# A decoder layer on one core: output projection and second feed-forward product by one level of Strassen's scheme

## The chip, the cores and the metric
One core of a Trainium2 chip runs the whole program. The metric is the device time of one execution in microseconds (us), the median of several runs. Engines: PE (TensorE, the matrix engine; its weight loads are listed as PEld), DVE (VectorE), ACT (ScalarE), POOL (GpSimd), SP (SyncE, which issues nearly all DMAs here).

## The reference, cut to what matters
One layer (DEPTH = 1) of a decoder with 512 tokens, model width 1024 and feed-forward width 4096, all in float32:
```
h = rms_norm(x, norm1_g)
A, B, C, D = four mixers of h, each of width 512
merged = sum over the four of sigmoid(gate_i(h)) * (mixer_i @ w_branch[i])    # 512 x 1024
x = x + merged @ w_out                                                        # output projection, 1024 x 1024
h2 = rms_norm(x, norm2_g)
x = x + relu(h2 @ w_ff1)**2 @ w_ff2                                           # 1024 x 4096, then 4096 x 1024
```
The change touches the last three lines only.

## The kernel before, in words
**Three matmuls for one.** A float32 operand is split into a rounded part (hi) and a rest (lo): ACT copies it into the rounded type (line 84), DVE subtracts that from the original (line 85; with a factor lines 88 and 89). `mm3` then issues hi*hi, hi*lo and lo*hi, the lines 143 to 145. Every one of these matmuls has 128x128 stationary weights and 512 moving columns.

**Weights.** `plan` lists all weight units in the order of use. A unit is 128x1024 numbers (512 KB). `load_raw` issues its DMA on SP into a ring of three `raw` tiles, `load_w` splits it into rings of three `whi` and three `wlo` tiles, and `wunit` hands the next one to PE, with the split two units and the DMA five units ahead. A unit feeds 24 matmuls.

**Order of the queues.** The program is written for a tile framework. It places each engine's instructions by a plan of its own, in which what was written first goes first unless it is not ready and something later is; waits and buffers are derived from the tiles. So the written order is not exactly the order on an engine's queue: the loads of x for the residual (line 1129), which are written behind the last branch, are issued while that branch runs.

**The stages that the change touches,** in the order of time:
- `branch(3)`: the last of four branches adds to the eight `merged` tiles (128 channels x 512 tokens each). The product is gated on DVE (line 828), and POOL adds it (line 832).
- Output projection: the eight `merged` tiles are halved and split into `mT` (lines 88 and 89). `gemm_a` runs twice, once for each half c of the 1024 output channels: stationary mT, moving w_out, four PSUM banks, one for each 128 tokens t; 2 x 8 x 4 x 3 = 192 matmuls. DVE adds the banks to the residual x2 (line 1138). The sum is transposed on PE (line 175), scaled by norm2_g and split into `xT`; ACT sums its squares (line 1144).
- First product (FF1): 32 units of `gemm_b`, each with 24 matmuls into one bank (128 of 4096 channels x 512 tokens): 768 matmuls. Then relu on ACT (line 1153) and the square on DVE (line 1154) into the tile `y`.
- Second product (FF2): two passes c over all 32 `y`, each with 16 units. Before a unit two `y` are split into `yy`; 2 x 4 x 3 matmuls accumulate in four banks over the whole pass; 768 matmuls in all. At the end of a pass DVE scales by the row's rms factor and adds x2 (line 1174), and SP writes the rows out.

**Memory.** `yy`, `mg` (merged) and `tg` lie in the pool `pg`, which is allocated from the right end of the memory, as are `xp` and `dnp` before it; all else lies in pools on the left.

Of the kernel before, what the change touches and what calls it, by code (L numbers as in the profile page):

```python
# [11 lines left out]
F32 = mybir.dt.float32  # L12
# [9 lines left out]
P = 128  # L22
S = 512
# [15 lines left out]
def trunk(ctx, tc, x, positions, norm1_g, w_in, dn_conv_w, dn_a_log, dn_dt_bias, dn_out_norm_g,  # L39
# [66 lines left out]
    def load_raw(i):  # L106
        while len(raws) <= min(i, len(plan) - 1):
            srcs, n, width = plan[len(raws)]
# [4 lines left out]
            raws.append(raw)  # L113

    def load_w(i):
        while len(wts) <= min(i, len(plan) - 1):
            j = len(wts)
            load_raw(j)
            used = plan[j][1] * plan[j][2]
            hi = wp.tile([P, 1024], F32R, tag="whi", name="whi")  # L120
            lo = wp.tile([P, 1024], F32R, tag="wlo", name="wlo")
            split(hi[:, :used], lo[:, :used], raws[j][:, :used])
            wts.append((hi, lo))
# [18 lines left out]
    def mm3(ps, lh, ll, rh, rl, start, stop):  # L142
        T.matmul(out=ps, lhsT=lh, rhs=rh, start=start, stop=False)  # L143
        T.matmul(out=ps, lhsT=lh, rhs=rl, start=False, stop=False)  # L144
        T.matmul(out=ps, lhsT=ll, rhs=rh, start=False, stop=stop)  # L145

# [34 lines left out]
    def mm4(lhsT, rhs):  # L181
# [163 lines left out]
    plan += plan_branch(3)  # L345
    for c in range(2):
        plan += spec_a(w_out[0], [(c * 512, 512)])
    for m in range(32):
        plan += spec_b(w_ff1[0], m * P)
    for c in range(2):  # L350
        for u in range(16):
            plan += spec_a(w_ff2[0, u * 256:(u + 1) * 256], [(c * 512, 512)], 2)
    load_w(AHEAD - 1)
# [765 lines left out]
    mT = []
    for k in range(KC):  # L1120
        hi, lo = WR("m", ("G", "V", "R", "U")[k // 2])
        split_scaled(hi, lo, merged[k], 0.5)
        mT.append((hi, lo))
    x2 = []
# [7 lines left out]
    ss2 = small([NT, 2], "ss2")  # L1132
    xb = [[up.tile([P, 4, S], F32R, tag="h", name="xT", bufs=4) for _ in range(2)] for _ in range(2)]
    xT = [tuple(xb[k // 4][i][:, k % 4, :] for i in range(2)) for k in range(KC)]
    for c in range(2):
        banks = gemm_a(512, mT)
        for t in range(NT):
            V.tensor_tensor(out=x2[t][c], in0=x2[t][c], in1=banks[t], op=ALU.add)
        for k in range(4):
            pb = tpose([x2[t][c][:, tsl(k)] for t in range(NT)])  # L1140
            split_scaled(*xT[c * 4 + k], pb, par(R_G2 + c * 4 + k))
        for t in range(NT):
            s_ = W("sq")
            A.activation(out=s_, in_=x2[t][c], func=AF.Square, accum_out=ss2[:, t, c:c + 1])
    r2 = small([NT], "rstd2")
    V.tensor_tensor(out=r2, in0=ss2[:, :, 0], in1=ss2[:, :, 1], op=ALU.add)
    V.tensor_scalar(out=r2, in0=r2, scalar1=1.0 / D, scalar2=EPS, op0=ALU.mult, op1=ALU.add)
    V.reciprocal(out=r2, in_=r2)
    ys = []
    for m in range(32):  # L1150
        ps, = gemm_b(xT)
        y = W("y", "AQSSGVRU"[m // 4])
        A.activation(out=y, in_=ps, func=AF.Relu)
        V.scalar_tensor_tensor(out=y, in0=ps, scalar=0.0, in1=y, op0=ALU.max, op1=ALU.mult)  # L1154
        ys.append(y)
    for c in range(2):
        cs_ = slice(c * 512, (c + 1) * 512)
        banks = [gbank() for _ in range(NT)]
        for u in range(16):
            hi, lo = wunit()  # L1160
            yy = []
            for kk in range(2):
                yh, yl = (pg.tile([P, S], F32R, tag="mg", name="yy", bufs=8) for _ in range(2))
                split(yh, yl, ys[u * 2 + kk])
                yy.append((yh, yl))
            order = [(kk, t) for kk in range(2) for t in range(NT)]
            if u == 15:
# [40 lines left out]
```

## Time and profile before
| | us |
|---|---|
| median of 3 runs | 1054.85 |
| lowest and highest run | 1054.62, 1056.58 |
| span of the profiled execution, first to last instruction | 1054.5 |
| PE busy in it | 1031.2 |
| DVE, ACT, POOL busy | 533.2, 401.3, 171.5 |

The profiled execution is known by its span; the median of the runs lies 0.4 us above it. A PE that is busy all the time can still be slowed, since the ends of its matmuls are modelled: what counts is the distance from the start of one matmul to that of the next.

### The profile page before, as it was taken

How to read it: one execution, taken by the hardware profiler on the slowest of the kernel's cores; microseconds unless marked ns; L12 is line 12 of the kernel's file. 1: busy time of each engine (PE TensorE's matmuls, PEld its weight loads, DVE VectorE, ACT ScalarE, POOL GpSimd, SP SyncE). 2: the span in 40 equal slices, each digit the busy share in tenths (PEclk: the TensorE clock that was granted, in tenths of full speed). 3: DMA queues.
4: the chain of work that ended last, by engine and by line, in shares of the span. 5: the costliest groups of instructions: out<-in, count | busy, mean ns of one | idle time of the engine just before them, and what ended most of it. 6: DMA issues, size and time to landing. Idle time of an engine off the chain costs nothing.

```text
span 1054.5 us, 13053 instructions
## 1 busy us (share of the span) xinstructions
PE 1031.2 (98%) x5067; PEld 847.4 (80%) x5067; DVE 533.2 (51%) x894; ACT 401.3 (38%) x700; POOL 171.5 (16%) x206
## 2 busy tenths in 40 slices
PE   7989999999999999999999999999999999999998
PEld 6868777888888767778888888888888888888886
DVE  6884899523645854442556334354333334445443
ACT  6572333332434442443444233343222223434331
POOL 2453234100300610104342212000000000000000
PEclk9999989999999999999999999999999999999999
DMA  6334342222233222222422333323333322324221
GB/s 196 102 100 119 91 94 67 81 60 80 71 85 99 76 80 80 61 79 77 126 61 79 121 91 90 99 82 98 100 100 100 94 90 98 100 87 133 100 80 40
DMA packets 130886, 96.71 MB, mean 92 GB/s; under 512 B 15924, under 2 KB 112256, under 8 KB 130824
## 3 DMA queue, kind: packets, MB, share of 16 engines
q1 hardware_dynamic: 130744, 95.85, 31.4%
q8 instruction: 40, 0.66, 0.2%
q14 instruction: 22, 0.18, 0.1%
q10 hardware_dynamic: 80, 0.03, 0.0%
HBM read 92.96 MB, written 2.90 MB: 91 GB/s over the span
## 4 chain that ended last, share of the span: by engine, by line
PE 86%; DVE 8%; issue 2%; DMA 1%; ACT 1%; POOL 1%; SPq 0%; DVEq 0%; ACTq 0%; POOLq 0%
PE g L143 25%; PE g L145 25%; PE g L144 25%; PE m L879 2%; PE m L175 1%; DVE wlo L85 1%; PE m L184 1%; PE m L1025 1%; DVE cv L516 1%; PE m L869 1%; PE m L1093 1%; PE m L1024 1%; DVE D L626 1%; DVE h L89 1%; DMA x<-in_x_dram 1%
## 5 line engine op out<-in xcount | busy, mean ns | idle before, releaser
L85 DVE TENSOR_TENSOR wlo<-raw,whi 128x1024 fp32r<-128x1024 f32 (+2 forms) x160 | 204.8, 1280 | 305.4 <-ACT whi L84 296.1
L84 ACT ACTIVATE whi<-raw 128x1024 fp32r<-128x1024 f32 (+2 forms) x160 | 167.8, 1048 | 368.6 <-PE g L144 235.1
L143 PE MATMUL g<-h,whi 128*128 128x512 f32 x416 | 168.0, 404 | 0.0
L145 PE MATMUL g<-h,wlo 128*128 128x512 f32 x416 | 164.2, 395 | 0.0
L144 PE MATMUL g<-h,whi 128*128 128x512 f32 x416 | 163.6, 393 | 0.0
L144 PE MATMUL g<-wlo,yy 128*128 128x512 f32 x256 | 101.1, 395 | 0.0
L145 PE MATMUL g<-whi,yy 128*128 128x512 f32 x256 | 101.1, 395 | 0.0
L143 PE MATMUL g<-whi,yy 128*128 128x512 f32 x256 | 101.0, 395 | 0.0
L143 PE MATMUL g<-xT,whi 128*128 128x512 f32 x256 | 99.7, 389 | 0.0
L144 PE MATMUL g<-xT,whi 128*128 128x512 f32 x256 | 99.6, 389 | 0.0
L145 PE MATMUL g<-xT,wlo 128*128 128x512 f32 x256 | 99.6, 389 | 0.0
L145 PEld LDWEIGHTS g<-h,wlo 128*128 128x128 f32 x416 | 79.0, 190 | 16.7
L143 PEld LDWEIGHTS g<-h,whi 128*128 128x128 f32 x416 | 79.1, 190 | 16.2 <-issue 0.5
L144 PEld LDWEIGHTS g<-h,whi 128*128 128x128 f32 x416 | 78.9, 190 | 16.1 <-issue 0.5
L85 DVE TENSOR_TENSOR yy<-y,yy 128x512 fp32r<-128x512 f32 x64 | 44.2, 691 | 82.1 <-ACT yy L84 81.7
L84 ACT ACTIVATE yy<-y 128x512 fp32r<-128x512 f32 x64 | 40.4, 631 | 107.2 <-PE g L144 101.5
L832 POOL TENSOR_TENSOR mg<-mg,tg 128x512 f32<-128x512 f32 x24 | 35.7, 1488 | 194.2 <-DVE tg L828 152.8
L145 PEld LDWEIGHTS g<-whi,yy 128*128 128x128 f32 x256 | 48.0, 187 | 11.8
L143 PEld LDWEIGHTS g<-whi,yy 128*128 128x128 f32 x256 | 48.0, 187 | 11.8 <-DVE y L1154 0.2
L144 PEld LDWEIGHTS g<-wlo,yy 128*128 128x128 f32 x256 | 48.0, 187 | 11.6
L143 PEld LDWEIGHTS g<-xT,whi 128*128 128x128 f32 x256 | 48.1, 188 | 10.0
L145 PEld LDWEIGHTS g<-xT,wlo 128*128 128x128 f32 x256 | 48.1, 188 | 10.0
(361 smaller groups left out, 1668.3 us busy)
## 6 DMA issues: line engine op xcount, KB each, us to landing
raw<-in_w_in_dram SPq DMA_DIRECT2D x68, 512.0 KB
raw<-in_w_ff_dram SPq DMA_DIRECT2D x64, 512.0 KB
raw<-in_w_branch_dram SPq DMA_DIRECT2D x16, 512.0 KB
raw<-in_w_out_dram SPq DMA_DIRECT2D x8, 512.0 KB
x<-in_x_dram SPq DMA_DIRECT2D x4, 512.0 KB
x<-in_x_dram SPq DMA_DIRECT2D x8, 256.0 KB
out_dram<-x SPq DMA_DIRECT2D x8, 256.0 KB
raw<-in_w_in_dram SPq DMA_DIRECT2D x4, 456.0 KB
```

The costliest lines, as they stand in the source:

```text
L84: A.activation(out=hi, in_=src, func=AF.Copy)
L85: V.tensor_tensor(out=lo, in0=src, in1=hi.bitcast(F32), op=ALU.subtract)
L89: V.scalar_tensor_tensor(out=lo, in0=src, scalar=sc, in1=hi.bitcast(F32), op0=ALU.mult, op1=ALU.subtract)
L143: T.matmul(out=ps, lhsT=lh, rhs=rh, start=start, stop=False)
L144: T.matmul(out=ps, lhsT=lh, rhs=rl, start=False, stop=False)
L145: T.matmul(out=ps, lhsT=ll, rhs=rh, start=False, stop=stop)
L175: T.transpose(out=pb[:, tsl(t)], in_=srcs[t], identity=ident)
L184: T.matmul(out=pb[:, tsl(t)], lhsT=lhsT[:, tsl(t)], rhs=rhs[:, tsl(t)], start=True, stop=True)
L516: V.scalar_tensor_tensor(out=y[:, 3 - k:], in0=ps[:, :n], scalar=par(R_CONV + 12 * k + blkno), in1=y[:, 3 - k:], op0=ALU.mult, op1=ALU.add)
L626: V.tensor_reduce(out=XB[:, r, m0:], in_=xr.rearrange("p c m -> p m c"), axis=AX.X, op=ALU.add, negate=True)
L832: G.tensor_tensor(out=merged[m], in0=merged[m], in1=tgs[b], op=ALU.add)
L879: T.matmul(out=pv[:, tsl(m)], lhsT=vblk(h, j), rhs=pts[n][:, o_ + j * P:o_ + (j + 1) * P], start=(j == 0), stop=(j == i))
```

## The change
**Strassen's scheme (Winograd's form).** The left matrix is cut into 2 x 2 (tokens 0 to 255 and 256 to 511; even and odd blocks of 128 channels), the right one too (even and odd blocks of 128 rows; column halves of 512). Seven products of the parts, and of sums of the parts, take the place of eight. This is done for the output projection (one group `gO`) and for FF2 cut into four blocks of 1024 rows (groups `gF[0]` to `gF[3]`). Each product p runs in two halves f of its 512 rows: a group has 14 units, and a unit has 2 x 2 x 3 = 12 matmuls (24 before).

**Sums.** All sums of parts run on POOL in float32, before the splits: `w_src` forms four sums of weights for each f (128 x 1024 numbers each), `a_sums` three sums of the left matrix and `a_split` a fourth (128 x 512 each). ACT and DVE split the weights of each unit as before (128 x 1024) and, new, the left part for each unit (128 x 512). After product 6 DVE forms u2 and u3 from PSUM, and POOL adds them into six tiles of x2 (128 x 512). The products 2, 5, 4 and 3 are added from PSUM by DVE, two tiles each.

**Order.** The plan of units alternates: the first eight FF1 units, then for each block three units of the block and one of FF1, four times, then the block's last two units and four of FF1. The fourth block's 14 units stand alone at the end. The 14 units of the projection stand alone too. The weights of a group come as four DMAs of 1 MB into tiles of a new pool `fp`, which takes the place of the pool `up` after the last branch; there is nothing of the projection's sums and splits ahead of the last branch's instructions in the text (`fence`).

**Other parts.** x2 is multiplied by the mean square on POOL (eight tiles) while FF1 runs and by its reciprocal on ACT at the end, so that blocks can add to it at any time. The split left parts lie in `fp`, on the left. The right pools get a pad of 32 bytes each, after which their tiles start at multiples of 64 bytes.

```diff
     def load_w(i):
-        while len(wts) <= min(i, len(plan) - 1):
+        while len(wts) <= min([i, len(plan) - 1] + fence):
             j = len(wts)
             load_raw(j)
+            load_t(j)
...
+            if srcs_w[j] is not None:
+                split(hi.rearrange("p (q c) -> p q c", c=512), lo.rearrange("p (q c) -> p q c", c=512), srcs_w[j])
+                wts.append((hi, lo) + a_split(*plan[j]))
+                continue
...
         load_w(i + AHEAD)
+        load_t(i + AHEAD + 1)
         load_raw(i + AHEAD + AHEAD_RAW)
...
+    PRODS = (1, 7, 6, 2, 5, 4, 3)
+    UNITS = [(1, 0), (7, 0), (1, 1), (7, 1)] + [(p, f) for p in PRODS[2:] for f in range(2)]
...
+    def wload(g, e):
+        for f in range(2):
+            t = fps[0].tile([P, 2, 1024], F32, tag="r" + "eo"[e], name="r" + "eo"[e], bufs=2)
+            SY.dma_start(out=t, in_=g["w"][f * 512:(f + 1) * 512].rearrange("(q e p) c -> e p q c", e=2, p=P)[e])
+            g["eo"[e]].append(t)
+
+    def w_src(g, p, f):
+        e, o = g["e"][f], g["o"][f]
+        b11, b12, b21, b22 = e[:, :, 0:512], e[:, :, 512:1024], o[:, :, 0:512], o[:, :, 512:1024]
+        if p == 7:
+            g["T3"][f] = fps[0].tile([P, 2, 512], F32, tag="T3", name="T3", bufs=2)
+            G.tensor_tensor(out=g["T3"][f], in0=b22, in1=b12, op=ALU.subtract)
+            return g["T3"][f]
+        if p == 6:
...
+            G.tensor_tensor(out=g["T2"][f], in0=g["T3"][f], in1=b11, op=ALU.add)
+            return g["T2"][f]
+        if p == 5:
+            G.tensor_tensor(out=b12, in0=b12, in1=b11, op=ALU.subtract)
+            return b12
+        if p == 4:
+            G.tensor_tensor(out=g["T2"][f], in0=b21, in1=g["T2"][f], op=ALU.subtract)
+            return g["T2"][f]
+        return {1: b11, 2: b21, 3: b22}[p]
+
+    def a_sums(g, f):
...
+        G.tensor_tensor(out=s1, in0=a21, in1=a22, op=ALU.add)
+        G.tensor_tensor(out=a21, in0=a11, in1=a21, op=ALU.subtract)
+        G.tensor_tensor(out=s2, in0=s1, in1=a11, op=ALU.subtract)
...
+    def a_split(g, p, f):
+        y = g["y"][f]
+        if p == 3:
+            G.tensor_tensor(out=g["S2"][f], in0=y[:, :, 1, 0:256], in1=g["S2"][f], op=ALU.subtract)
...
+        ah, al = (fps[0].tile([P, 2, 256], F32R, tag="a" + n, name="a" + n, bufs=4) for n in "hl")
...
+    def wunit_mm(g, p, f, dst, last=None):
+        hi, lo, ah, al = wunit()
...
+        for q in range(2):
+            for t in range(2):
+                mm3(X[t], ah[:, q, tsl(t)], al[:, q, tsl(t)], hi[:, q * 512:(q + 1) * 512],
+                    lo[:, q * 512:(q + 1) * 512], not more and f + q == 0, f + q == 2, more)
...
+            for t in range(2):
+                V.tensor_tensor(out=u[2][t], in0=u[2][t], in1=X[t], op=ALU.add)
+                V.tensor_tensor(out=u[3][t], in0=u[2][t], in1=g["X"][3][t], op=ALU.add)
+            for t in range(2):
+                for d, v in ((dst(2 + t, 1), u[3][t]), (dst(2 + t, 0), u[2][t]), (dst(t, 1), u[2][t])):
+                    G.tensor_tensor(out=d, in0=d, in1=v, op=ALU.add)
...
+    pad(xp, "padx")
...
+    seq = [m for m in range(8)]
+    for i in range(4):
+        us = list(UNITS)
+        for m in range(4 * (i < 3)):
+            seq += [(i,) + us.pop(0) for _ in range(3)] + [8 * i + 8 + m]
+        seq += [(i,) + v for v in us] + [8 * i + 12 + m for m in range(4 * (i < 3))]
...
+    up.release()
+    fps.append(ctx.enter_context(tc.tile_pool(name="fp", bufs=1, reuse_waits="tile")))
+    for e in range(2):
+        wload(gO, e)
...
+    gO["y"] = mgs
+    for f in range(2):
+        a_sums(gO, f)
+    fence.clear()
+    load_w(pos[0] + AHEAD - 1)
+    for p, f in UNITS:
+        wunit_mm(gO, p, f, lambda t, c: x2[t][c])
+        if (p, f) == (3, 0):
+            x2t(0)
...
+            G.tensor_scalar(out=x2[t][c], in0=x2[t][c], scalar1=ms2[:, t:t + 1], scalar2=None, op0=ALU.mult)
...
+    def finish(t, c, ps):
+        A.activation(out=x2[t][c], in_=x2[t][c], func=AF.Copy, scale=r2[:, t:t + 1])
+        V.scalar_tensor_tensor(out=x2[t][c], in0=ps, scalar=r2[:, t:t + 1], in1=x2[t][c], op0=ALU.mult, op1=ALU.add)
+        SY.dma_start(out=out[0, tsl(t), c * 512:(c + 1) * 512], in_=x2[t][c])
...
+            if i < 3 and f == 1 and p in (5, 3):
+                wload(gF[i + 1], int(p == 3))
```

## Rows read from the trace of the kernel before

**Rows 1.** The page: busy times, the granted clock and the DMA rate in 40 slices
```profile
PE 1031.2 (98%) x5067; PEld 847.4 (80%) x5067; DVE 533.2 (51%) x894; ACT 401.3 (38%) x700; POOL 171.5 (16%) x206
...
PEclk9999989999999999999999999999999999999999
...
GB/s 196 102 100 119 91 94 67 81 60 80 71 85 99 76 80 80 61 79 77 126 61 79 121 91 90 99 82 98 100 100 100 94 90 98 100 87 133 100 80 40
```
**Rows 2.** Busy times by stage: projection, FF1, FF2 (stretch, its length, then the engines)
```profile
core 0: us, PE busy (x) PEld busy (x) DVE busy (x) ACT busy (x) POOL busy (x), PEclk, DMA share, GB/s
649.70:695.20 45.50, 45.50 (x210) 37.73 (x209) 18.83 (x22) 16.07 (x27) 2.14 (x1) 1.00 0.32 91
696.90:870.90 174.00, 174.00 (x770) 144.09 (x769) 63.40 (x74) 53.16 (x72) 0.00 (x0) 1.00 0.33 97
870.90:1050.40 179.50, 179.50 (x770) 143.88 (x769) 83.60 (x98) 67.06 (x91) 0.00 (x0) 1.00 0.27 89
```
**Rows 3.** Matmuls by tile (ns min/median/max, first and last start): FF1's, FF2's, projection's
```profile
L143 PE MATMUL g<-xT,whi x256: 389/389/486, 696.9 to 870.5; 128*128 128x512 f32 x128
...
L143 PE MATMUL g<-whi,yy x256: 393/395/407, 871.2 to 1049.7; 128*128 128x512 f32 x128
...
L143 PE MATMUL g<-whi,mh x64: 389/389/477, 649.7 to 694.5; 128*128 128x512 f32 x64
```
**Rows 4.** The chain that ended last, between the projection and FF1
```profile
671.64 1.87 PE m L175 x16
...
695.31 1.88 PE m L175 x16
```
**Rows 5.** Groups by line and shape, 580 us to the end (busy us, mean ns)
```profile
L85 DVE TENSOR_TENSOR wlo<-raw,whi 128x1024 fp32r<-128x1024 f32 x82 | 101.4, 1237 | 165.4 <-ACT whi L84 165.4
...
L84 ACT ACTIVATE whi<-raw 128x1024 fp32r<-128x1024 f32 x82 | 86.5, 1055 | 164.3 <-PE g L144 124.0 <-issue 21.5 <-PE g L145 18.6
...
L85 DVE TENSOR_TENSOR yy<-y,yy 128x512 fp32r<-128x512 f32 x64 | 44.2, 691 | 82.1 <-ACT yy L84 81.7 <-PE g L144 0.4
L84 ACT ACTIVATE yy<-y 128x512 fp32r<-128x512 f32 x64 | 40.4, 631 | 107.2 <-PE g L144 101.5 <-DVE y L1154 5.6
...
L1138 DVE TENSOR_TENSOR x<-x,g 128x512 f32<-128x512 f32 x8 | 5.3, 683 | 2.5 <-PE g L145 2.5
```
**Rows 6.** POOL's largest groups by shape, whole span
```profile
L832 POOL TENSOR_TENSOR mg<-mg,tg 128x512 f32<-128x512 f32 x24 | 35.7, 1488 | 194.2 <-DVE tg L828 152.8 <-issue 41.0 <-DVE rqm L993 0.4
...
L1099 POOL TENSOR_SCALAR E<-Fb,gcc 128x512 f32<-128x512 f32 x4 | 7.2, 1806 | 0.0
```
**Rows 7.** POOL in order of time around 600 us (start, length)
```profile
599.01 1.29 POOL L832 TENSOR_TENSOR mg<-mg,tg 128x512 f32<-128x512 f32 x1 [14.61 <-DVE tg L828]
602.36 2.20 POOL L832 TENSOR_TENSOR mg<-mg,tg 128x512 f32<-128x512 f32 x1 [2.07 <-DVE tg L828]
```
**Rows 8.** DVE in order of time in the same stretch
```profile
601.60 0.68 DVE L828 SCALAR_TENSOR_TENSOR tg<-tg,g 128x512 f32<-128x512 f32 x1
602.20 1.22 DVE L85 TENSOR_TENSOR wlo<-raw,whi 128x1024 fp32r<-128x1024 f32 x1
```
**Rows 9.** POOL, then DVE, around 324 us
```profile
324.39 1.29 POOL L832 TENSOR_TENSOR mg<-mg,tg 128x512 f32<-128x512 f32 x1 [1.38 <-DVE tg L828]
...
324.50 2.26 DVE L85 TENSOR_TENSOR wlo<-raw,whi 128x1024 fp32r<-128x1024 f32 x1 [0.19 <-ACT whi L84]
```
**Rows 10.** POOL, then DVE, around 59 us (line 516 reads one operand from PSUM)
```profile
59.05 1.36 POOL L569 TENSOR_TENSOR UA<-UA,br 128x512 f32<-128x512 f32 x1 [3.90 <-ACT UA L568]
...
59.43 0.74 DVE L516 SCALAR_TENSOR_TENSOR cv<-g,prm,cv 128x511 f32<-128x511 f32 x1
```
**Rows 11.** SP's queue in order of time, 586 to 628 us
```profile
589.39 1.29 SPq L1129 DMA_DIRECT2D x<-in_x_dram  x3
...
619.76 0.37 SPq L112 DMA_DIRECT2D raw<-in_w_branch_dram  x1
624.84 0.37 SPq L112 DMA_DIRECT2D raw<-in_w_out_dram  x1
```
**Rows 12.** The end: the last matmul and the last work of DVE
```profile
1050.15 0.39 PE L145 MATMUL g<-whi,yy 128*128 128x512 f32 x1
...
1050.58 0.75 DVE L1174 SCALAR_TENSOR_TENSOR x<-g,rstd,x 128x512 f32<-128x512 f32 x1 [0.65 <-PE g L145]
```

More of the change, by code (lines that the diff above doesn't have):

```diff
@@ L138, in wunit, with mm3 @@
         load_w(i + AHEAD)
+        load_t(i + AHEAD + 1)
         load_raw(i + AHEAD + AHEAD_RAW)
         return wts[i]
[L142 to L145, printed above, removed]
+    def mm3(ps, lh, ll, rh, rl, start, stop, more=False):
+        T.matmul(out=ps, lhsT=lh, rhs=rh, start=start, stop=False, skip_group_check=more)
+        T.matmul(out=ps, lhsT=lh, rhs=rl, start=False, stop=False, skip_group_check=more)
+        T.matmul(out=ps, lhsT=ll, rhs=rh, start=False, stop=stop, skip_group_check=more)
     def gemm_b(xs, nb=1):
@@ new lines, in wunit_mm @@
+    def wunit_mm(g, p, f, dst, last=None):
+        hi, lo, ah, al = wunit()
+        x = XOF[p]
+        more = p in (2, 4, 3)
+        if not more and f == 0:
+            g["X"][x] = [gbank() if x in (2, 4) else mbank() for _ in range(2)]
+        X = g["X"][x]
+        for q in range(2):
+            for t in range(2):
+                mm3(X[t], ah[:, q, tsl(t)], al[:, q, tsl(t)], hi[:, q * 512:(q + 1) * 512],
+                    lo[:, q * 512:(q + 1) * 512], not more and f + q == 0, f + q == 2, more)
+        if f == 0:
+            return
+        u = g["u"]
+        if p == 1:
+            u[2] = [fps[0].tile([P, 512], F32, tag="u", name="u", bufs=4) for _ in range(2)]
+            for t in range(2):
+                A.activation(out=u[2][t], in_=X[t], func=AF.Copy)
+        elif p == 6:
+            u[3] = [fps[0].tile([P, 512], F32, tag="u", name="u", bufs=4) for _ in range(2)]
+            for t in range(2):
+                V.tensor_tensor(out=u[2][t], in0=u[2][t], in1=X[t], op=ALU.add)
+                V.tensor_tensor(out=u[3][t], in0=u[2][t], in1=g["X"][3][t], op=ALU.add)
+            for t in range(2):
+                for d, v in ((dst(2 + t, 1), u[3][t]), (dst(2 + t, 0), u[2][t]), (dst(t, 1), u[2][t])):
+                    G.tensor_tensor(out=d, in0=d, in1=v, op=ALU.add)
+        elif p != 7:
+            r, c = {2: (0, 0), 5: (2, 1), 4: (2, 0), 3: (0, 1)}[p]
+            for t in range(2):
+                d = dst(r + t, c)
+                if last is None:
+                    V.tensor_tensor(out=d, in0=d, in1=X[t], op=ALU.add)
+                else:
+                    last(r + t, c, X[t])
@@ L187, in trunk, with pad @@
+    def pad(pool, name):
+        G.memset(pool.tile([P, 8], F32, name=name, bufs=1), 0.0)
     W0 = w_in[0]
@@ L345, in trunk @@
     plan += plan_branch(3)
[L346 to L352, printed above, removed]
+    gO = wgroup(w_out[0], 0.5)
+    gF = [wgroup(w_ff2[0, i * 1024:(i + 1) * 1024]) for i in range(4)]
+    fence.append(len(plan) - 1)
+    plan += [(gO, p, f) for p, f in UNITS]
+    seq = [m for m in range(8)]
[4 more added lines that the diff above has]
+        seq += [(i,) + v for v in us] + [8 * i + 12 + m for m in range(4 * (i < 3))]
+    for e in seq:
+        plan += spec_b(w_ff1[0], e * P) if isinstance(e, int) else [(gF[e[0]], e[1], e[2])]
     load_w(AHEAD - 1)
@@ L744, in trunk @@
     pg = tc.alloc_tile_pool(name="pg", bufs=4, side="right")
+    mgs = [pg.tile([P, 2, 2, S], F32, tag="mg", name="mg", bufs=2) for _ in range(2)]
     OB = [W("ob", "U") for _ in range(H)]
@@ L1117, in trunk @@
     branch(3, oD, drain=True)
[L1119 to L1123, printed above, removed]
+    pad(pg, "padg")
+    up.release()
+    fps.append(ctx.enter_context(tc.tile_pool(name="fp", bufs=1, reuse_waits="tile")))
+    for e in range(2):
+        wload(gO, e)
     x2 = []
@@ L1142, in trunk @@
         for t in range(NT):
-            s_ = W("sq")
+            s_ = fps[0].tile([P, S], F32, tag="u", name="sq", bufs=4)
             A.activation(out=s_, in_=x2[t][c], func=AF.Square, accum_out=ss2[:, t, c:c + 1])
[L1145 to L1155, printed above, removed]
@@ L1177, in trunk @@
-    pg.release()
+    gO["y"] = mgs
[7 more added lines that the diff above has]
+            x2t(0)
+    for e in range(2):
+        wload(gF[0], e)
+    x2t(1)
+    pg.release()
+    py = tc.alloc_tile_pool(name="py", bufs=3, side="right", reuse_waits="tile")
+    mr = small([2, NT], "rstd2")
+    ms2, r2 = mr[:, 0, :], mr[:, 1, :]
+    V.tensor_tensor(out=ms2, in0=ss2[:, :, 0], in1=ss2[:, :, 1], op=ALU.add)
@@ new lines, in trunk @@
+    for e in seq:
+        if isinstance(e, int):
+            g, f, q = gF[e // 8], e // 4 % 2, e % 4
+            if q == 0:
+                g["y"].append(py.tile([P, 2, 2, S], F32, tag="y", name="y", bufs=3))
+                if e == 0:
+                    pad(py, "pady")
+            ps, = gemm_b(xT)
+            y = g["y"][f][:, q // 2, q % 2, :]
+            A.activation(out=y, in_=ps, func=AF.Relu)
+            V.scalar_tensor_tensor(out=y, in0=ps, scalar=0.0, in1=y, op0=ALU.max, op1=ALU.mult)
+            if q == 3:
+                a_sums(g, f)
+        else:
+            i, p, f = e
+            wunit_mm(gF[i], p, f, lambda t, c: x2[t][c], finish if i == 3 else None)
+            if i < 3 and f == 1 and p in (5, 3):
+                wload(gF[i + 1], int(p == 3))
```

66 lines of the change are left out of this document (37 added, 29 removed).

## The prediction

> **What bounds the kernel now.** I read the page first: PE is busy for 98% of the span at the full granted clock, DVE for half of it, POOL for 16% [rows 1]. Then the table by stage: the projection takes 45.5 us, FF1 174.0 and FF2 179.5, with PE busy throughout and DVE at 41%, 36% and 47% [rows 2]. So all three stages are as long as their matmuls. For the price of one I took starts, not lengths: FF1's 256 matmuls of one line start from 696.9 to 870.5 us, 765 matmuls further on, which makes 0.2269 us each. FF2's start from 871.2 to 1049.7, which makes 0.2333 [rows 3]. The two differ in the operand held in PE: `yy` in the right pool. The projection, whose `mh` lies on the left, runs at FF1's pace: 192 x 0.2269 = 43.6, and 1.87 for 16 transposes amid it [rows 4] make its 45.5 us. Last I read what the added work will meet: POOL and DVE side by side [rows 7 to 10].
>
> **PE: what is removed.** The projection goes from 192 to 168 matmuls, FF2 from 768 to 4 x 168 = 672. The held operand of both now lies on the left, so I price all at 0.2269. A group of 14 units is 38.1 us. Projection with its transposes: 40.0 (-5.5). FF2: 152.5 (-27.0). If the pace of 0.2333 stayed, FF2 would be 4.3 us longer. By PE alone the change is worth 32.5 us.
>
> **DVE and ACT: what is added.** A unit now has half the matmuls, 2.72 us, and the same weight split. DVE takes 1.24 for the weights and 0.69 for the left part, ACT 1.06 and 0.63 [rows 5]: 1.93 and 1.69 in 2.72 us. Alone, both keep up. The 12 additions from PSUM of a group take 0.68 each [rows 5], 8.2 us.
>
> **POOL: what is added.** A group has 8 sums of 128x1024 and 14 of 128x512 (8 of the left matrix, 6 into x2). One of 128x512 with two inputs takes 1.29 us undisturbed [rows 7]. None of 128x1024 was run: at most twice that, 2.58, and at least twice the 1.15 that remains below when start-up is hidden, 2.30. The Trainium skill (GPSIMD Engine Reference, section 3.1) gives 2.6 cycles an element, by which I estimate 2.2 us; the sums of a group would be under 1 us shorter by it.
>
> **DVE and POOL together.** This is where the sum is decided. POOL's addition took 1.29 us at 599.01 and 2.20 at 602.36 [rows 7], when DVE's split had begun 0.16 us earlier and ended at 603.42 [rows 8]: POOL ran 1.14 us after that end. The other way round, DVE's split began at 324.50 in POOL's addition (324.39 to 325.68) and took 2.26 us, to 326.76 [rows 9]: 1.08 after POOL's end. So these two kinds of instruction, both with two inputs from SBUF, take turns. A DVE instruction with one input from PSUM is not held: 0.74 us within POOL's 1.36 [rows 10]. The Trainium skill (SBUF, section "Who interferes with whom") says the same: DVE with at most one SBUF input does not contend. The trace agrees, so the additions from PSUM are left out below; if they took turns too, a group would be 8.2 us longer.
>
> The price of a turn, net of start-up: 1.08 for a weight split, 0.56 for a left part (0.69 less the same 0.14), 1.15 and 2.30 for POOL's sums. A group: DVE 14 x 1.64 = 23.0, POOL 8 x 2.30 + 14 x 1.15 = 34.5, together 57.5 us of a path that is used by one at a time, against 38.1 on PE. Whether that shows depends on what else PE has.
>
> *Projection.* PE has nothing else: FF1 needs x2. Before the last branch ends little can be done: the left sums of f=0 and the split of the first unit; the other tiles of `fp` lie on the last branch's operands. After it POOL holds 14 sums whose inputs are there (the last merge, 3 left sums, 8 of weights, 2 for product 3): 8 x 2.30 + 6 x 1.15 = 25.3. If each takes turns with one DVE split, only 7 units (11.5) are split after 36.8 us. Then the six additions into x2 (6.9) alternate with three more units (4.9): 48.6. Four units remain for DVE alone (4 x 1.93 = 7.7) with about six additions from PSUM between (4): 60.3. The last unit's matmuls: 63.0 us, that is +17.5 on 45.5. Bounds: turns packed without loss, (34.5 + 1.15 - 3.45) + (23.0 - 1.64) + 2.7 = 56.3 (+10.8); turns that cost nothing, 40.0 and 3 for the start (-2.5); full lengths one after another, 36.1 + 25.1 + 8.2 + 2.7 = 72.1 (+26.6). I take 63: POOL is always ready early, and nothing makes it wait for DVE.
>
> *To FF1.* PE's 16 transposes and FF1's start remain; the last bank must first be added on DVE, which I put at +1 (0 to 3). The mean-square products on POOL (8 x 1.81 [rows 6] = 14.5 us) run in FF1's first eight units (43.6 us), where POOL has little else; uncovered they would cost their length.
>
> *Blocks 0 to 2.* Each has 8 FF1 units beside it: PE 38.1 + 43.6 = 81.7, shared path 57.5 + 8 x 1.08 = 66.1, 81% full. A split may start only when its buffer, three units back, is free, so some come late; I take 1.5 us a block, 4.5 in all. Bounds: 0, and two units a block that wait for one long sum, 2 x 2.3 x 3 = 14.
>
> *Block 3.* No FF1 beside it. Ahead of it are its six left sums (6.9), two weight sums (4.6) and three units (4.9): 57.5 - 16.4 = 41.1 remain, with the last matmuls and a late split some 45 us against 38.1: +6.9. Bounds: 0, and nothing ahead, 60.2 (+22.1).
>
> *DMA and tail.* The bytes are the same; loads come as 1 MB. SP's last load before w_out is issued at 619.76, and it issued loads that are written later already at 589 [rows 11], so 4 MB for the projection, at the 196 GB/s that the first slice shows [rows 1] 21 us, land before 649. Later groups have at least four FF1 units (21.8 us) for their last 2 MB. Uncovered, 1 MB costs 5.3. From the last matmul to the end it was 4.4 us [rows 12]; two tiles instead of one are left then, and ACT's product is done before: 0.
>
> **The sum,** on the span of 1054.5: +17.5 + 1 + 4.5 - 27.0 + 6.9 = +2.9, 1057.4; the median lay 0.4 above the span, so **1058**. The sign hangs on one number: the projection must end within 45.5 + 14.6 = 60.1 us for a gain.
>
> **Rivals.**
> - *Packed turns* (the other side). POOL and DVE still take turns, but no turn falls where PE waits for more than the sum: projection 56.3, blocks 0 to 2 unhindered, block 3 at 41.1. +10.8 + 1 - 27.0 + 3.0 = -12.2, 1043. It decides once the projection is under 60.1. For it: POOL is idle for 84% of the span, and the queues are ordered by readiness [rows 1, 11]. Against it: in the projection all sums are ready at once.
> - *No collision.* The sums find gaps, PE alone decides: -2.5 + 1 - 27.0 = -28.5, 1026. Against it stand both pairs above [rows 7 to 9].
> - *FF1 used up as filler.* PE takes FF1 units ahead whenever a split is late, and block 3 is left with the whole shared path: 52 instead of 45, and 3 us of stall in each earlier block more: +2.9 + 7 + 9, about 1074.
> - *Clock.* Gaps in the projection, where PE works 40 of 63 us, lower the granted clock, which fell only in the first slices [rows 1]. A unit at 1.2 GHz would take 5.4 instead of 2.7 us; with half the units so and half of that behind waits, +9: 1067.
>
> **How the numbers follow.** The forecast (1050 to 1066, its own range) 0.38, packed turns 0.27, no collision 0.12, FF1 as filler 0.13, clock 0.10. No change I can tell is within 0.2% (2.1 us, about what a measurement of this kernel can tell). Slower: 0.23 of the forecast's share and the last two rivals, 0.46; the same: 0.08; faster: 0.07 of the forecast and the first two rivals, 0.46. The 8-in-10 range leaves out most of "no collision" and the far end of "filler": 1034 to 1075.
>
> **What the profile of the changed kernel would show.** Right: 168 matmuls and over 60 us from the last branch to the transposes of c=1; DVE's splits there at 2 to 3.5 us each, ended by POOL's sums; POOL's 128x1024 sums at 2.3 us alone and over 3 in company; FF2's matmuls 0.227 us apart; block 3 some 45 us. Wrong if DVE's splits keep their 1.24 us while POOL works, if the projection is under 56 us, or if PE runs FF1 matmuls amid a block's units so that block 3 is far over 45.

## The result, and the profile after

The changed kernel takes 1086.18 us (median of 4 runs, 1084.36 to 1092.46), the kernel before 1055.45 in the same comparison: ratio 1.0305, 95% interval 1.0286 to 1.0325. Forecast were 1058 and a range up to 1075. The profiled execution has a span of 1082.6 us, 28.1 more than before.

The page of the changed kernel, to be read against [rows 1]:
```profile
PE 1017.7 (94%) x4947; PEld 830.7 (77%) x4947; DVE 672.3 (62%) x966; ACT 437.5 (40%) x746; POOL 410.4 (38%) x328
...
PEclk9999999999999999999999996899999999999899
...
GB/s 195 96 96 127 97 98 60 78 59 78 78 88 97 78 59 78 59 98 117 78 59 117 97 214 0 35 180 94 24 117 136 59 76 177 39 40 195 19 1 78
```
PE did get less to do (120 matmuls fewer in the records), yet the span grew: 65 us without a busy PE where there were 23. The granted clock falls in the slices of the projection, and the DMA rate goes from 214 just before it through 0 and 35 to 180 GB/s.

The same by stage: the projection (from the last branch's end to FF1's first matmul), the first eight FF1 units, block 0 with four FF1 units between its units, the four FF1 units behind its end, the same two rows of block 1, the four FF1 units behind block 2, and block 3:
```profile
core 0: us, PE busy (x) PEld busy (x) DVE busy (x) ACT busy (x) POOL busy (x), PEclk, DMA share, GB/s
648.25:720.30 72.05, 49.03 (x185) 36.24 (x185) 55.78 (x45) 29.16 (x43) 48.63 (x25) 0.83 0.17 60
720.30:765.75 45.45, 45.45 (x210) 37.60 (x208) 26.44 (x29) 18.58 (x30) 32.65 (x17) 1.00 0.33 95
765.75:825.90 60.15, 60.09 (x265) 49.40 (x264) 49.46 (x45) 28.76 (x37) 30.65 (x15) 1.00 0.33 107
825.90:854.20 28.30, 24.12 (x98) 19.16 (x98) 12.98 (x12) 6.74 (x10) 14.87 (x8) 0.94 0.25 72
854.20:914.30 60.10, 60.09 (x266) 49.27 (x265) 49.45 (x45) 28.64 (x37) 30.81 (x15) 1.00 0.33 107
914.30:942.50 28.20, 24.12 (x98) 19.15 (x97) 12.82 (x12) 6.75 (x10) 14.71 (x8) 0.94 0.25 71
...
1002.50:1031.70 29.20, 24.40 (x98) 19.39 (x98) 13.62 (x12) 6.70 (x10) 15.49 (x8) 0.88 0.06 17
1031.70:1078.90 47.20, 41.60 (x169) 32.01 (x167) 38.41 (x35) 23.49 (x32) 24.14 (x13) 0.96 0.09 34
```
The surprise is where PE waits. Amid the interleaved blocks it never does: 264 matmuls in 60.1 us. It waits where four FF1 units stand in a row, plain work that the scheme does not touch: 28.3, 28.2 and 29.2 us for 96 matmuls that take 21.8 at FF1's pace. Against the prediction:

| us | predicted | measured | off by |
|---|---|---|---|
| projection and transposes, to FF1 (47.2 before) | +18.5 | 72.05 + 1.9 - 47.2 - 1.45 = +25.3 | 6.8 |
| PE work of FF2 | -27.0 | -26.75 | 0.2 |
| blocks 0 to 2 | +4.5 | 0.5 amid the units; 6.5 + 6.4 + 7.4 in the four FF1 units: +20.8 | 16.3 |
| block 3 | +6.9 | 47.2 - 38.1 = +9.1 | 2.2 |
| tail | 0 | 3.7 - 4.0 = -0.3 | -0.3 |
| sum | +2.9 | +28.1 | 25.2 |

(1.9 are the transposes of c=1, which now run behind FF1's first matmuls; 1.45 is how much earlier the last branch ends in this execution. The 26.75 are reckoned: FF1 and FF2 took 353.5 us [rows 2], and 1440 matmuls at FF1's pace take 326.75; what the blocks took beyond that stands in their rows.)

The prices of single instructions came out as forecast. DVE's and POOL's groups by shape, 580 us to the end, against [rows 5, 6]:
```profile
L86 DVE TENSOR_TENSOR wlo<-raw,whi 128x1024 fp32r<-128x1024 f32 x42 | 84.0, 2006 | 47.0 <-ACT whi L85 46.6
...
L86 DVE TENSOR_TENSOR al<-y,ah 128x512 fp32r<-128x512 f32 x32 | 34.3, 1071 | 45.4 <-ACT ah L85 45.4
...
L291 DVE TENSOR_TENSOR x<-x,m 128x512 f32<-128x512 f32 x16 | 10.2, 677 | 0.0
```
```profile
L230 POOL TENSOR_TENSOR re<-re 128x1024 f32<-128x1024 f32 x10 | 32.1, 3215 | 0.0
...
L223 POOL TENSOR_TENSOR T<-ro,re 128x1024 f32<-128x1024 f32 x10 | 24.3, 2434 | 71.7 <-DMA ro<-in_w_ff_dram 71.7
...
L249 POOL TENSOR_TENSOR S<-y,S 128x512 f32<-128x512 f32 x8 | 15.6, 1976 | 4.9 <-DVE al L86 4.9
```
DVE's split of 128x1024 takes 2.01 us on average for the 42 units from `raw` and 1.78 over all 112, where it took 1.24; the addition from PSUM keeps its 0.68. POOL's large sum takes 2.4 us undisturbed, within the bounds of 2.30 to 2.58. By the 2.6 cycles an element of the Trainium skill (GPSIMD Engine Reference, section 3.1) I had estimated 2.2 us; the trace is about a tenth above it. But the row of line 223 has another number: POOL sat idle for 71.7 us ahead of four such sums, waiting for a load of `ro`.

One of the four waits, in the order of time of POOL, of SP's queue and DVE, of ACT, and of PE:
```profile
820.48 2.40 POOL L223 TENSOR_TENSOR T<-ro,re 128x1024 f32<-128x1024 f32 x1 [19.84 <-DMA ro<-in_w_ff_dram]
...
829.53 2.40 POOL L223 TENSOR_TENSOR T<-ro,re 128x1024 f32<-128x1024 f32 x1
831.88 1.29 POOL L241 TENSOR_TENSOR S<-y 128x512 f32<-128x512 f32 x1
...
835.48 1.29 POOL L242 TENSOR_TENSOR y<-y 128x512 f32<-128x512 f32 x1
```
```profile
815.23 2.85 SPq L215 DMA_DIRECT2D ro<-in_w_ff_dram  x2
```
```profile
813.93 1.23 DVE L86 TENSOR_TENSOR wlo<-ro,whi 128x1024 fp32r<-128x1024 f32 x1 [0.26 <-ACT whi L85]
...
823.89 0.68 DVE L1301 SCALAR_TENSOR_TENSOR y<-g,y 128x512 f32<-128x512 f32 x1
```
```profile
823.43 1.06 ACT L85 ACTIVATE whi<-raw 128x1024 fp32r<-128x1024 f32 x1 [1.40 <-PE g L162]
836.80 0.63 ACT L85 ACTIVATE ah<-y 128x512 fp32r<-128x512 f32 x1 [12.31 <-POOL y L242]
837.34 1.99 ACT L85 ACTIVATE whi<-raw 128x1024 fp32r<-128x1024 f32 x2
```
```profile
838.43 0.50 PE L160 MATMUL g<-xT,whi 128*128 128x512 f32 x1 [1.44 <-ACT whi L85]
...
841.91 0.50 PE L162 MATMUL g<-xT,wlo 128*128 128x512 f32 x1 [2.74 <-DVE wlo L86]
...
843.04 0.63 PE L162 MATMUL g<-xT,wlo 128*128 128x512 f32 x1
843.47 0.63 PE L160 MATMUL g<-xT,whi 128*128 128x512 f32 x1
```
Read it from below. PE waits for the weights of an FF1 unit. Their split (837.34) starts 13.9 us after the weight split before it (4.2 us in run 5 below); it stands on ACT's queue behind the split of a left part for the next block, which waits 12.31 us for POOL's sum a21 (835.48). That sum's `y` was ready at 824.6, but stands on POOL's queue behind five weight sums of the next block, whose first waits for a 1 MB load; and that load was issued at 815.23 only, when DVE had read block 0's rows out of the first of the two `ro` buffers (813.93). PE needs none of this before block 1, 18 us later. The order is the framework's plan, not the text's: there the left sums come first.

The waits are not the whole price. Behind the second one PE's matmuls start 0.43 us apart (843.04, 843.47) in place of 0.227; the granted clock from 842.5 to 845.5 us is 0.50, which is 1.2 GHz. So of the 20.3 us that the three rows of four FF1 units lose, 13.1 are waits and about 7 the pace behind them.

In the projection PE first waits 10.1 us, from 648.4 to 658.5, with a similar order on ACT and, behind it, on POOL:
```profile
658.46 1.22 PE L160 MATMUL m<-whi,ah 128*128 128x512 f32 x2 [10.08 <-ACT whi L85]
```
```profile
656.83 0.63 ACT L89 ACTIVATE ah<-mg 128x512 fp32r<-128x512 f32 x1 [4.75 <-POOL mg L242]
657.36 1.04 ACT L85 ACTIVATE whi<-re 128x1024 fp32r<-128x1024 f32 x1
```
```profile
657.98 2.80 POOL L223 TENSOR_TENSOR T<-ro,re 128x1024 f32<-128x1024 f32 x1
667.04 1.29 POOL L249 TENSOR_TENSOR S<-mg,S 128x512 f32<-128x512 f32 x1 [6.27 <-DVE al L90]
668.27 3.36 POOL L227 TENSOR_TENSOR T<-T,re 128x1024 f32<-128x1024 f32 x1
```
The first unit's weights (657.36) are split behind four left parts. POOL is later idle for 6.27 us ahead of a sum that only the last product needs, with the sums for the next products behind it.

So there were two theories. **A**: DVE and POOL take turns, and the sum of their work is the path; it was only longer than I made it. **B**: nothing is short of time, but in-order queues hold instructions that wait ahead of others that could run.

### The profile page after: what moved, and what is told of

It reads as the page before. It is cut to its first block, busy times and chain, and to the rows that moved or that the text cites. A ratio compares the mean times of both kernels' runs of the same rounds, so it can differ in the third digit from the quotient of the medians.

```text
span 1082.6 us, 13015 instructions
## 1 busy us (share of the span) xinstructions
PE 1017.7 (94%) x4947; PEld 830.7 (77%) x4947; DVE 672.3 (62%) x966; ACT 437.5 (40%) x746; POOL 410.4 (38%) x328
## 4 chain that ended last, share of the span: by engine, by line
PE 64%; DVE 15%; POOL 8%; issue 7%; DMA 3%; ACT 2%; SPq 0%; POOLq 0%; DVEq 0%; ACTq 0%
PE g L162 16%; PE g L160 16%; PE g L161 16%; DVE wlo L86 6%; POOL T L223 2%; PE m L998 2%; PE m L161 2%; PE m L160 1%; PE m L162 1%; PE m L192 1%; POOL T L227 1%; POOL re L230 1%; PE m L201 1%; DVE al L86 1%; PE m L1144 1%
## 5 line engine op out<-in xcount | busy, mean ns | idle before, releaser
L86 DVE TENSOR_TENSOR wlo<-raw,whi 128x1024 fp32r<-128x1024 f32 (+1 forms) x120 | 187.5, 1565 | 185.0 <-ACT whi L85 175.2
L85 ACT ACTIVATE whi<-raw 128x1024 fp32r<-128x1024 f32 (+1 forms) x120 | 125.2, 1046 | 275.5 <-PE g L161 160.8
L160 PE MATMUL m<-whi,ah 128*128 128x512 f32 x160 | 64.6, 407 | 14.8 <-ACT whi L85 14.8
L161 PE MATMUL m<-wlo,ah 128*128 128x512 f32 x160 | 65.3, 408 | 6.7 <-DVE wlo L86 6.7
L86 DVE TENSOR_TENSOR wlo<-T,whi 128x1024 fp32r<-128x1024 f32 x30 | 48.7, 1625 | 30.4 <-ACT whi L85 30.2
L162 PE MATMUL m<-whi,al 128*128 128x512 f32 x160 | 64.1, 401 | 0.0
L86 DVE TENSOR_TENSOR al<-y,ah 128x512 fp32r<-128x512 f32 x32 | 34.3, 1071 | 45.4 <-ACT ah L85 45.4
L160 PEld LDWEIGHTS g<-xT,whi 128*128 128x128 f32 x256 | 49.2, 192 | 16.1 <-ACT whi L85 6.1
L285 POOL TENSOR_TENSOR x<-x,u 128x512 f32<-128x512 f32 x30 | 51.7, 1761 | 17.5 <-DVE u L281 17.5
L161 PEld LDWEIGHTS g<-xT,whi 128*128 128x128 f32 x256 | 49.3, 193 | 10.6 <-DVE xT L90 0.2
L161 PE MATMUL g<-wlo,ah 128*128 128x512 f32 x120 | 48.2, 402 | 7.1 <-DVE wlo L86 7.1
```

Of the source, the lines that this page charges most:

```text
L85: A.activation(out=hi, in_=src, func=AF.Copy)
L86: V.tensor_tensor(out=lo, in0=src, in1=hi.bitcast(F32), op=ALU.subtract)
L160: T.matmul(out=ps, lhsT=lh, rhs=rh, start=start, stop=False, skip_group_check=more)
L161: T.matmul(out=ps, lhsT=lh, rhs=rl, start=False, stop=False, skip_group_check=more)
L162: T.matmul(out=ps, lhsT=ll, rhs=rh, start=False, stop=stop, skip_group_check=more)
L285: G.tensor_tensor(out=d, in0=d, in1=v, op=ALU.add)
```

## The experiments

There are fourteen more kernels; each ratio is to the kernel before, timed alongside. "Stage" is the projection from the last branch's end to FF1's first matmul, 47.2 us before and 72.1 in the changed kernel; "stretch" the four FF1 units in a row.

**1. No sums.** `w_src` and `a_split` hand out raw parts in place of sums.
```diff
-            G.tensor_tensor(out=g["T3"][f], in0=b22, in1=b12, op=ALU.subtract)
-            return g["T3"][f]
+            return b12
...
```


> The changed kernel without its 64 sums on POOL: products and their splits take the raw parts in place of the sums (the output is not the reference's); order, units, loads, pads, the adds to x2 and everything on PE stay. If the loss comes from the sums alone (their time on POOL, DVE's turns with them, and what waits behind them), PE meets no more than a few us of new idle time: 32.5 us of matmuls gone from 1054.85 and some 3 to 8 us of waits at the stage borders, 1025 to 1031. Rival: the alternation of FF1 and block units, the 1 MB loads or the units of 12 matmuls cost by themselves; then it stays above 1050.

1034.99 us (0.9797, interval 0.9778 to 0.9816), 4 us above the forecast; stage 48.7, stretches without a stall. The sums (they are 80, not the 64 of the text above), with all that they make wait, cost some 50 us. Of the 32.5 us of matmuls 21.3 are gained; the other 11 go to what stayed (units, loads, alternation, the adds to x2), and this run does not part them.

**2. Left sums on DVE.**
```diff
-        G.tensor_tensor(out=s1, in0=a21, in1=a22, op=ALU.add)
+        V.tensor_tensor(out=s1, in0=a21, in1=a22, op=ALU.add)
...
```


> The 40 sums of the left parts (128x512) run on DVE in place of POOL; the same arithmetic. Theory A (DVE and POOL share their turns, and the sum of their work is what PE waits for): the work only changes place, within 4 us of the changed kernel's 1086, since a sum costs DVE at least half of what POOL took. Theory B (an instruction that waits at the head of an in-order queue: the left sums stand on POOL behind weight sums that wait for a load, and ACT's splits of FF1's weights stand behind the split of the left part): the three stretches of four FF1 units fall from 28.2 us to 22 to 23.5 and the time to 1066 to 1074; the start of the projection gains at most 3.

1081.31 (1.0240, 1.0225 to 1.0255): outside both ranges and nearer to A's, against the reading above. The trace says why it tells little: DVE's own plan put these sums behind a split of late FF1 weights, into the burst of POOL's weight sums, where each took 2.2 to 2.9 us and the splits of FF1's weights stood behind them. The stretch kept 27.8 us.

**3. Order pinned as written.** Every weight sum (POOL) and left split (ACT, DVE; all in the form with a factor, 1.0 in the second product) passes through
```diff
+    def KP(g, ins):
+        if True:
+            tc.keep_in_program_order(ins)
...
```


> Nothing but the order of three queues changes: every weight sum on POOL, and every split of a left part on ACT and DVE, is pinned behind what is written before it. Theory A (turns): the same work in another order, 1080 to 1090. Theory B (heads of queues): the left sums no longer stand behind a weight sum that waits for its load, nor the weight splits behind left parts that are not ready: the stretches of four FF1 units fall to 22 to 24 us (-13 to -18), PE's idle time at the start of the projection from 10.3 us to 3 to 6; in all 1058 to 1070. What speaks against a full gain: weight sums issued only three units ahead may come late in blocks.

1118.02 (1.0583, 1.0564 to 1.0602), far off both. The stretches did lose their stalls, and PE's first wait in the projection went (first matmul at 648.0, not 658.5), but the stage stayed at 70.8: as far as this run shows, that wait was slack of a longer path. And weight sums that are issued only three units ahead came late inside the blocks: the sums of product 5 stood behind the six adds to x2 (9 us), and PE waited for `ah` up to 5 us at a time. Order costs as much the other way; this run is no test of A.

**4. Second product alone** in the new form, the projection with `mT` as before.
```diff
...
-    for p, f in UNITS:
-        wunit_mm(gO, p, f, lambda t, c: x2[t][c])
+    for c in range(2):
+        banks = gemm_a(512, mT)
+        for t in range(NT):
+            V.tensor_tensor(out=x2[t][c], in0=x2[t][c], in1=banks[t], op=ALU.add)
...
```


> The output projection as in the kernel before (merged split into mT, two passes of 96 matmuls), the second feed-forward product as in the changed kernel. Both theories: the 26.6 us that the projection stage lost come back, less what FF1's first units lose: 1057 to 1063. If the loss of the projection was only moved time (something that FF1 or the blocks wait for anyway), more than 1070.

1063.69 (1.0073, 1.0056 to 1.0091), just above the range. The second product alone loses too, all of its 27 us of matmuls and more.

**5, 6. One constraint:** T3 of a block's first half behind that half's left sums, on the full change and on the kernel of 4.
```diff
+            t3 = G.tensor_tensor(out=g["T3"][f], in0=b22, in1=b12, op=ALU.subtract)
+            if f == 0 and g is not gO:
+                tc.keep_in_program_order(t3)
```


> The changed kernel with one constraint on POOL's queue: the first weight sum of each block of the second product (T3 of the first half, which waits for a load) stands behind the left sums of the same half. Theory B (left sums late behind that wait, and with them ACT's splits of FF1's weights): the three stretches of four FF1 units fall from 28.2 us to 22 to 23.5, in all 1066 to 1072. Theory A (DVE's splits doubled in length by POOL's burst of weight sums, whoever is first): the burst stays where it is, the stretches keep 27 us or more, 1082 to 1088.

> The projection as before (mT), the second product in blocks, and the same constraint on POOL's queue as in the run on the full change. Theory B: 1063.7 less 14 to 20, so 1044 to 1050. Theory A: 1060 to 1065.

1067.62 (1.0110, 1.0093 to 1.0127) and 1043.47 (0.9880, 0.9865 to 0.9895). POOL's order, ACT's, and a stretch of the first (columns as above):
```profile
826.73 1.29 POOL L243 TENSOR_TENSOR S<-y 128x512 f32<-128x512 f32 x1 [22.84 <-DVE y L1303]
828.10 2.16 POOL L244 TENSOR_TENSOR y<-y 128x512 f32<-128x512 f32 x1
...
831.48 6.19 POOL L223 TENSOR_TENSOR T<-ro,re 128x1024 f32<-128x1024 f32 x2
```
```profile
830.29 0.63 ACT L85 ACTIVATE ah<-y 128x512 fp32r<-128x512 f32 x1 [2.55 <-POOL y L244]
830.83 1.04 ACT L85 ACTIVATE whi<-raw 128x1024 fp32r<-128x1024 f32 x1
```
```profile
829.20:851.10 21.90, 21.90 (x98) 18.15 (x97) 16.40 (x11) 6.97 (x10) 20.92 (x8) 1.00 0.27 76
```
The same work, POOL busy for 20.9 of 21.9 us, but the left sums first: ACT's wait is 2.55 in place of 12.31 us, and all three stretches take 21.9 to 22.0, at a granted clock of 1.00. B is shown for the stretches: 20 us, the lower clock behind the waits included.

**7. Projection alone** in the new form, the second product as before.
```diff
...
-    for e in seq:
-        plan += spec_b(w_ff1[0], e * P) if isinstance(e, int) else [(gF[e[0]], e[1], e[2])]
+    for m in range(32):
+        plan += spec_b(w_ff1[0], m * P)
+    for c in range(2):
+        for u in range(16):
+            plan += spec_a(w_ff2[0, u * 256:(u + 1) * 256], [(c * 512, 512)], 2)
...
```


> The projection by Strassen's scheme as in the changed kernel, the second product as before (two passes of 16 units, yy in a pool that starts at a multiple of 64 bytes). If the two halves of the change add up: the projection stage 26 us longer, the second product 5 us shorter by the pace 0.227 us for 0.2333 us per matmul: 1074 to 1080. If the late projection delays loads or weights of FF1 too, more.

1079.56 (1.0212, 1.0193 to 1.0231), +23.2. With the 3.3 us that the pads give the old second product here (run 8) the projection costs 26.5; with run 4's 7.4 that makes 34, the full change 31. The halves add up to within 3 us.

**8. The pads alone** in the kernel before.
```diff
+    pad(xp, "padx")
...
+    pad(dnp, "padd")
...
+    pad(pg, "padg")
```


> The kernel before with nothing but 32 bytes of pad in each pool at the right end, so that their tiles start at multiples of 64 bytes. If the pace of the second product (0.2333 us per matmul before, 0.227 in the changed kernel's blocks) comes from where yy lies: 768 matmuls by 0.0064 us, 4.9 us less, 1049 to 1052. If it comes from something else (the two passes, DVE's traffic): 1054 to 1057.

1053.20 (0.9967, 0.9954 to 0.9980), between the two. FF2's rows, against [rows 3]:
```profile
L143 PE MATMUL g<-whi,yy x256: 387/388/464, 869.1 to 1044.3; 128*128 128x512 f32 x128
```
765 matmuls in 175.2 us are 0.2290 each, 0.2333 before: two thirds of the difference to FF1 is where `yy` lies.

**9, 10. The projection's sums,** on the kernel of 5 (1067.62): all on DVE, or only the sum for product 3 later on POOL.
```diff
+    def E(g):
+        return V if g is gO else G
...
-            G.tensor_tensor(out=g["T2"][f], in0=g["T3"][f], in1=b11, op=ALU.add)
+            E(g).tensor_tensor(out=g["T2"][f], in0=g["T3"][f], in1=b11, op=ALU.add)
```
```diff
+            s4 = G.tensor_tensor(out=g["S2"][f], in0=y[:, :, 1, 0:256], in1=g["S2"][f], op=ALU.subtract)
+            if g is gO:
+                tc.keep_in_program_order(s4)
```


> The change with the constraint on POOL's queue (1067.6), and all sums of the projection's group (8 of weights, 8 of left parts) on DVE in place of POOL; the six adds to x2 stay on POOL. Theory A (turns: every sum on POOL costs DVE its whole length): the sums take DVE some 8 x 1.24 + 8 x 0.69 = 15 us in place of 28 on POOL, so the projection stage falls from 72 to about 60 us, in all 1054 to 1060. Theory B (POOL's queue order alone made the projection late): the same direction, but as DVE's queue is also in order, 1060 to 1066. If neither sets the projection: 1065 to 1070.

> The change with the constraint on POOL's queue (1067.6), and in the projection's group the sum for product 3 (128x512, which waits for DVE's split of product 6) pinned on POOL behind what is written before it, so that the weight sums no longer stand behind it. Theory B (head of POOL's queue, 6.3 us of idle POOL at 661 us): 1061 to 1064. Theory A (sum of turns): the idle time only moves, 1065 to 1070.

1057.23 (1.0020, 1.0009 to 1.0032), stage 60.8; and 1062.82 (1.0081, 1.0054 to 1.0107), stage 68.0. Of the 72 us, 4 were the head of POOL's queue, as B says. 11, which may hold those 4, go when the sums leave POOL for DVE, an engine with more to do. The stage of run 9 in two parts, columns as above:
```profile
651.50:657.50 6.00, 0.09 (x2) 0.05 (x1) 5.85 (x8) 2.10 (x3) 1.64 (x1) 0.78 0.04 18
657.50:712.20 54.70, 47.63 (x184) 36.46 (x185) 48.39 (x53) 27.24 (x40) 10.98 (x7) 0.87 0.24 85
```
DVE now has 61 instructions in the stage, not 45, and is busy for 54.2 us, not 55.8: what turns no longer cost it pays for the sums. That speaks for A. But a sum is also shorter on DVE than on POOL, and these runs do not part the two.

**11, 12. The last block's sums, or all, on DVE,** old projection: 11 on the kernel of 6, 12 on that of 4 with no constraint. As in 9, with
```diff
...
+        return V if g is gF[3] else G
```
and for 12 with V in every case.

> The version with the old projection, the second product in blocks and the constraint on POOL's queue (1043.5), with the sums of the last block (8 of weights, 8 of left parts) on DVE in place of POOL. Theory A: in the last block, where FF1 gives no cover, each weight sum frees a turn of 2.3 us and takes 1.24: its 47 us fall to 41 to 44, in all 1038 to 1041. If DVE's queue order makes them late: 1043 to 1048.

> The old projection, the second product in blocks, and all sums of its four groups on DVE (POOL keeps the adds to x2 and the mean-square products); no constraint on any queue. DVE has then some 66 us of work in the 81.7 us of matmuls of a block with its eight FF1 units. Theory A: no turns but those with the adds: stretches of four FF1 units 22 to 24, last block 41 to 44, in all 1036 to 1042. Theory B (in-order queue, now DVE's, with sums that wait for a load ahead of splits): 1045 to 1060.

1038.16 (0.9841, 0.9820 to 0.9863) and **1036.87 (0.9833, 0.9808 to 0.9858), the lowest time of all**, though the two intervals overlap. One stretch of run 12 and its last block (47.20 us above), columns as in the table by stage, and its first weight sums on DVE:
```profile
805.30:827.20 21.90, 21.90 (x98) 18.16 (x97) 15.35 (x18) 7.10 (x10) 0.00 (x0) 1.00 0.35 96
990.20:1031.40 41.20, 39.15 (x169) 31.20 (x167) 36.49 (x42) 23.93 (x32) 9.96 (x6) 1.00 0.10 39
```
```profile
L226 DVE TENSOR_TENSOR T<-ro,re 128x1024 f32<-128x1024 f32 x8 | 9.8, 1220 | 9.0 <-DMA ro<-in_w_ff_dram 9.0
```
DVE has more instructions in the block (42, not 35) and is busy for less time (36.5, not 38.4 us). The sum that waits for `ro` now stands on DVE's queue, for 9.0 us in all, and no stretch stalls.

**13. Turns alone:** the kernel before, with sums on POOL that nothing reads.
```diff
...
+            if c == 0:
+                G.tensor_tensor(out=pt_[:, :, 0:512], in0=po_[:, :, 512:1024], in1=pe_[:, :, 512:1024], op=ALU.subtract)
+            else:
+                G.tensor_tensor(out=pe_[:, :, 512:1024], in0=pe_[:, :, 512:1024], in1=pe_[:, :, 0:512], op=ALU.subtract)
```


> The kernel before, with 32 sums of 128x1024 on POOL that nothing reads, issued one behind the other from the start of the second product (two tiles that FF1 left free are set to zero first). Nothing waits for them. Theory A (turns): each of DVE's three splits of a unit waits for one sum, a unit takes 3 x 2.30 and 1.08 + 2 x 0.56 = 9.1 us in place of 5.6 while the sums last, 32 sums for 10.7 units: +37 us, 1085 to 1097, with DVE's splits of 128x1024 at 3.4 us. Rival (only queue order cost time in the changed kernel; engines do not hold each other): 1053 to 1058, with these splits at 1.24 us.

1085.81 (1.0290, 1.0268 to 1.0311): 30 us for work that nobody waits for. DVE's groups while the sums run (869 to 963 us), and after:
```profile
L85 DVE TENSOR_TENSOR yy<-y,yy 128x512 fp32r<-128x512 f32 x21 | 56.1, 2704 | 2.6 <-ACT yy L84 2.6
L85 DVE TENSOR_TENSOR wlo<-raw,whi 128x1024 fp32r<-128x1024 f32 x11 | 37.5, 3408 | 3.6 <-ACT whi L84 3.6
```
```profile
L85 DVE TENSOR_TENSOR yy<-y,yy 128x512 fp32r<-128x512 f32 x38 | 26.2, 691 | 45.1 <-ACT yy L84 44.8 <-PE g L144 0.4
L85 DVE TENSOR_TENSOR wlo<-raw,whi 128x1024 fp32r<-128x1024 f32 x19 | 23.3, 1225 | 4.1 <-ACT whi L84 4.1
```
3.41 against 1.23, 2.70 against 0.69: each split waits for one sum, 2.0 to 2.2 us; 32 splits meet 32 sums. The Trainium skill (SBUF — State Buffer, section "Summary: rules for kernel authors") has the rule that of two such instructions the second to issue is blocked until the first finishes; the trace agrees, by these 2.0 to 2.2 us. Of the 30 us some 17 are PE's waits while the sums run; the granted clock of that stretch is 0.91.

**14. All sums of the full change on DVE,** as in 12.

> The full change (projection and second product) with every sum of its five groups on DVE; POOL keeps the adds to x2 and the mean-square products. Theory A: as the version with the old projection (1036.9), plus what the projection by this scheme takes more with its sums on DVE (60.7 us against 45.5, less 3 that its first matmuls start earlier): 1047 to 1053, a gain over the kernel before. Rival (the scheme's sums cost the same wherever they run): 1065 to 1085.

1046.95 (0.9919, 0.9900 to 0.9938), stage 60.7: a gain, but 10 us behind version 12. Even so the projection by this scheme loses 13.5 us of its own stage.

## Why the prediction was wrong

*What held.* PE's pace in the blocks (0.228 us a matmul, 0.227 assumed), the price of a turn (an estimated 3.4 for a split and a sum, 3.41 in run 13), POOL's 2.4 us, the addition from PSUM that is not held, x2's products hidden in FF1, the tail, and the danger named for the sign: the projection did not end within 60 us. That the projection's 4 MB landed before 649 was luck: SP issued them from 635.8 to 637.4, not near 620, and the DMA engines then moved 422 GB/s (640 to 645 us) where I had reckoned with 196.

*The step that failed* is "DMA and tail" together with "Blocks 0 to 2". I let a load be in time if PE needs its data later ("Later groups have at least four FF1 units (21.8 us) for their last 2 MB"), and took 1.5 us a block for splits whose buffer comes free late. But the load has a reader on an in-order queue, the weight sum on POOL, and that stands there with the next half's left sums behind it; and ACT's queue hands the delay on to FF1's weights. My bounds (0 to 14 us) did not hold the 20.8. Run 5 removes the wait by order alone and leaves some 2 us amid the blocks: with that queue order 4.5 would have been fair, and the 9.6 us by which its 1067.6 lies above the forecast are nearly the next two terms.

*Projection* (63, and 1 to FF1; measured 6.8 more): "POOL is always ready early, and nothing makes it wait for DVE" was wrong. POOL's sum for product 3 waited 6.3 us for DVE with the weight sums behind it; run 10 puts that at 4 us. The other 3 I have not taken apart; their cause stays open.

*Block 3* (45, measured 47.2): with the sums on DVE it takes 41.2, and DVE is busy for less time with more to do (run 12), so turns were in it as forecast. The size was 2 us low.

*The rivals.* "Clock" came true, and not in the projection alone. There the granted clock was 0.64 in the 10 us in which PE waited and 0.69 from 658.5 to 685.6 us (stretches at 1.2 and at 2.4 GHz), where PE waited for 8.6 of 27.1 us; 28 matmuls of the stage start about 0.43 us apart, 5.4 us more than at FF1's pace, and no run shows how much of that lay on the path. In the stretches it is about 7 of the 20 us. The forecast's sum had no term for it. "FF1 as filler" did not happen: PE kept the written order, FF1's units themselves were late. Its 1074 came nearest to the measured time, for a wrong reason. What I lacked was a rival for the queues' heads.

## What to carry to other kernels

A load is not hidden just because its last consumer is late; follow it to its first reader, and ask what stands behind that reader on its queue, and behind whoever waits for those. A wait of PE can cost more than its length: 13.1 us of waits in the stretches came with about 7 us of matmuls at the lower clock. Before moving elementwise sums to an idle POOL, price them as DVE time: a sum of 2.4 us on POOL held one of DVE's splits up for 2.0 to 2.2 us (run 13), and the same sum on DVE takes 1.22 (run 12). A scheme that trades matmuls for sums pays where other matmuls cover the sums (the second product, -1.7%) and not where PE has nothing else to do (the projection, +13.5 us at best here).

## What was not expected of the hardware

- 32 sums that nothing reads, on an engine that was idle, made the kernel 2.9% slower (run 13).
- The pace of the matmuls with `yy` as the held operand went from 0.2333 to 0.2290 us by 32 bytes of pad. FF1's pace is 0.2269; what makes the other 0.002 is open.
- POOL's sums of line 230 write over an operand and show 3.2 us on average, those of line 223 2.4. It is not the overwriting: in run 13 both kinds took 2.9 us in the same company of DVE.
